# A layer with 32 experts on one core: an expert's further block moves behind its first product, the general path's test moves to expert 29, PSUM banks and the seeding are laid anew

## The chip, the cores and the metric

The kernel runs on one core of a Trainium2 chip. The metric is the device time of one execution in microseconds; before the change the median of three runs is 1111.02 us (1110.48 to 1111.2). PE is TensorE, DVE is VectorE, ACT is ScalarE, POOL is GpSimd, and SP is the engine that here only issues DMAs.

## What is computed

One layer over 256 tokens of width 1024, in float32, with a context prefix of 256 tokens: a modulated norm, one input projection, four mixers side by side, an output projection with a residual (about the first 170 us), and then a mixture of experts. Cut to that second half:

```python
def moe(h, w_router, b_router, w_gu, b_gu, w_down, b_down):
    logits = h @ w_router + b_router
    top_vals, top_idx = lax.top_k(logits, 4)
    gates = jax.nn.softmax(top_vals, axis=-1)
    # for each of 32 experts e, over the tokens that chose it:
    gu = xb @ w_gu[e] + b_gu[e]                     # 1024 -> 2048
    gt = jnp.minimum(gu[:, :1024], 7.0)
    up = jnp.clip(gu[:, 1024:], -7.0, 7.0)
    y = ((up + 1) * gt * jax.nn.sigmoid(1.702 * gt)) @ w_down[e] + b_down[e]   # 1024 -> 1024
    # the sum over a token's four experts, weighted by its gates
x = x + g2 * moe(rmsnorm(x) * (1 + sc2) + sh2)
return rmsnorm(x, final_norm_g)
```

Each expert has 8 MB of `w_gu` and 4 MB of `w_down`, so 402 MB of weights pass through the core once.

## The kernel before

**The stream of weights.** An expert's weights are six units of 2 MB: u0 to u3 are `w_gu`, u4 and u5 are `w_down`. I number units through: unit 6e + u, up to expert 30, whose last unit is sent behind expert 31's first four. A ring of nine places in SBUF holds them. `load_unit` issues a unit's DMA from SP (L571 for `w_gu`, L581 for `w_down`), and `load_to(n)` issues all up to unit n. A unit may be issued when the one nine before it in the same place has been read for the last time; SP waits for that on PE's semaphore, and everything behind it in SP's order waits too. Units 0 to 8 first need what lies in their places from the first half of the kernel: unit 8 takes the place of `XT` and `YT`.

**One expert.** Every expert has room for 64 tokens (CAP). `gate_up(e)` (L961, L972) multiplies the picked tokens by units u0 to u3, two of its eight steps to a unit. `pick` (L930) gathers the next expert's tokens, `swiglu` works on DVE and ACT, `turn_rows` and `turn_act` (L939, L989) transpose, `s_pair` (L923) turns the gates, `scatter_part` (L1026) adds finished rows into the output banks `Y`, and `down(e)` (L961, L998) multiplies by u4 and u5 at the start of the next turn of the loop, L1109 following.

**More than 64 tokens.** `with tc.If(r > CAP)` (L1114) asks in each of the experts 0 to 29, on PE, DVE and ACT, whether there is a further block of 32 tokens; `block` computes it, and reads u0 to u3 (L1057) and u4, u5 (L1075) once more. It stands between `down(e - 1)` and `gate_up(e)`. Where it is skipped, each engine first lets its own earlier work finish and then adds all the counts of the skipped block to its semaphore in one go (on PE 92 of them), so that waits further on mean the same on both ways. With these inputs one expert takes it, expert 8.

**More than 96.** The general path (L1144 to L1169) loads an expert's weights again into six places of the ring and computes blocks until no token is left. Its test (L1149) stands at the end, behind `swiglu()` of expert 31, and it asks SP too. It is not taken here. Where it is skipped, SP waits for the landing of the DMAs whose semaphores it uses, and then adds its counts to them.

**Order and banks.** The order on each engine is that of the code. Before the first expert PE turns `XT` round twice: into banks that ACT scales to `H` (`natural`), and into the output banks `Y` (`seed`), in which the experts' results are then summed. `seed(1)` stands behind `turn_rows` of the first expert and is the last reader of `XT`, so unit 8 waits for it.

Of the kernel before, what the change touches and what calls it, by code (L numbers as in the profile page):

```python
# [9 lines left out]
AF = mybir.ActivationFunctionType  # L10
# [4 lines left out]
P = 128  # L15
D = 1024
# [6 lines left out]
MORE = 32  # L23
SLOT = 2048
# [45 lines left out]
def tile_hybrid_moe(tc, x, ctx, vec, mats, const, pos_col, pos_row, rows, bias, w_mod, w_in, w_out,  # L70
# [4 lines left out]
    with tc.tile_pool(name="big", bufs=1) as big, tc.tile_pool(name="acc", bufs=1, space=PSUM) as acc_pool, \  # L75
# [10 lines left out]
        def R(off, n):  # L86
            return B[:, off:off + n]
# [691 lines left out]
        N = [[bank[4 + 2 * c + q] for q in range(2)] for c in range(2)]  # L779
        Y = [[bank[2], bank[3]], [bank[6], bank[7]]]  # L780
# [7 lines left out]
        jk = R(O_ACC, 512)  # L788
        GT = R(O_GATE, 64).rearrange("p (c e) -> p c e", c=2)
# [15 lines left out]
        def natural(i):  # L805

            for c in range(2):
                pe.transpose(N[c][i // 4][:, (i % 4) * P:(i % 4 + 1) * P], XT[:, i, c * P:(c + 1) * P], ident)

        def seed(c):  # L810

            for i in range(KT):
# [7 lines left out]
        def squares(b, q, a, z):  # L820
            for c in range(2):
                act.activation(jk[:, a:z], N[c][q][:, a:z], AF.Square, scale=D ** -0.5, accum_out=ssq[:, b, c:c + 1])
# [8 lines left out]
        squares(0, 0, 0, 512)  # L831
# [5 lines left out]
        squares(1, 1, 0, 256)  # L837
# [10 lines left out]
        w2 = ssq[:, 0, :]  # L848
        dve.tensor_tensor(out=w2, in0=w2, in1=ssq[:, 2, :], op=ALU.add)
        rsqrt_newton(rs2, w2, tn2)  # L850
        act.activation(SM[:, 1:2], epsc, AF.Exp)
        for c in range(2):
            dve.scalar_tensor_tensor(LG[:, c, :], LR[:, c, :], rs2[:, c:c + 1], LB, op0=ALU.mult, op1=ALU.add)
            for q in range(2):
                act.activation(H[:, c, cols2[q]], N[c][q], AF.Copy, scale=rs2[:, c:c + 1])
            dve.max(out=M8[:, c, :], in_=LG[:, c, :])
        dve.tensor_scalar(nm, M8[:, :, 0], -1.0, None, op0=ALU.mult)
        dve.memset(M8[:, :, TOPK:8], 3.0e38)
        for c in range(2):
            dve.match_replace(out=MK[:, c, :], in_to_replace=M8[:, c, :], in_values=LG[:, c, :], imm_value=-3.0e38)  # L860
            act.activation(EX[:, c, :], LG[:, c, :], AF.Exp, bias=nm[:, c:c + 1])
        dve.tensor_tensor(out=MK, in0=MK, in1=LG, op=ALU.not_equal)
        dve.tensor_copy(MB, MK)
# [42 lines left out]
        G0, G1 = bank[4], bank[5]  # L906
        mis = [bank[0], bank[1]]
# [28 lines left out]
        def turn_rows(dst, ps):  # L936
# [4 lines left out]
            d4 = dst.rearrange("p j (g s) -> p j g s", g=2)  # L941
            dve.tensor_tensor(out=d4, in0=ps.rearrange("p (j g s) -> p j g s", j=4, g=2),  # L942
                              in1=jg(A2s).unsqueeze(3).to_broadcast([P, 4, 2, CAP]), op=ALU.mult)
            dve.tensor_tensor(out=d4, in0=d4, in1=jg(SH2s).unsqueeze(3).to_broadcast([P, 4, 2, CAP]), op=ALU.add)
# [139 lines left out]
        one_hot(0)  # L1084
# [18 lines left out]
        load_to(NPAIR)  # L1103

        parts = [(0, 0), (0, 1), (1, 0), (1, 1)]
        for e in range(NE - 1):
            pr, par = divmod(e, 2)
            if e < NE - 2:
                r = nc.values_load(CNT[0:1, e:e + 1], min_val=0, max_val=L, engines=engines)  # L1109
# [3 lines left out]
            if e < NE - 2:  # L1113
                with tc.If(r > CAP):  # L1114
                    block(e, CAP, G0, G1, GH, TH, UP)
# [5 lines left out]
            gate_up(e, XET)  # L1121
            if e == NE - 2:
                load_to(NE * NUN)
# [24 lines left out]

        with tc.If(r > CAP + MORE):  # L1149
            kept = dict(wt), dict(dn)  # L1150
            for e in range(NE):
                base = CAP if e >= NE - 2 else CAP + MORE
                r = nc.values_load(CNT[0:1, e:e + 1], min_val=0, max_val=L, engines=more)
                with tc.If(r > base):
                    for u in range(NUN):
                        load_unit(3 + u, e, u)
                    for b in range(base, L, MORE):
                        args = e, b, mis[0], mis[0], R(O_O, 512), R(O_O + 512, 512), R(O_XET, 512)
                        if b == base:
                            block(*args)  # L1160
                        else:
                            with tc.If(r > b):
                                block(*args)
            for now, old in zip((wt, dn), kept):
                now.update(old)
# [143 lines left out]
```

## Time and profile before

| | |
|---|---|
| median of three runs | 1111.02 us |
| the profiled execution, its own time | 1112.09 us |
| its span, first to last instruction | 1110.3 us |
| PE busy | 1025.7 us (92%) |
| DMA, mean over the span | 401 GB/s |
| read from HBM | 442.41 MB |

The page gives each engine's busy time, the span in 40 slices and the costliest groups of instructions. PE's 92% is a sum over overlapping matmuls and no proof that PE is the bound: a matmul of 512 columns in float32 is booked with about 0.6 us and the next one starts 0.21 us later. For this kernel the DMA line of the slices, the waits of SP and the timeline around single events tell more.

### The profile page before, as it was taken

Reading aid. Unit: us, or ns where it says so; the run is one execution under the profiler, and the core shown is the slowest. Engines: PE = TensorE matmul, PEld = TensorE weight load, DVE = VectorE, ACT = ScalarE, POOL = GpSimd, SP = SyncE. Lnnn points to the kernel's source line nnn. Section 1 sums busy time; section 2 is a strip of 40 time slices with the busy share of each in tenths; the row PEclk is TensorE's granted clock in tenths of the full one; section 3 lists DMA queues with packets and bytes.
Section 4 is the critical chain, followed back from the end, with each engine's and each line's share of the span. In section 5 each row is a group of like instructions: output and inputs, shape, how many; then the busy total and the mean of one; then the engine's idle time right before and its main releaser. Section 6 shows DMA issues by size and latency. Waiting matters only on the chain. (4 is left out here: it accounts for less than half of the span.)

```text
span 1110.3 us, 11952 instructions
## 1 busy us (share of the span) xinstructions
PE 1025.7 (92%) x4932; PEld 435.8 (39%) x4932; DVE 305.6 (28%) x593; ACT 128.5 (12%) x239; POOL 34.6 (3%) x77
## 2 busy tenths in 40 slices
PE   4999988999999989999999999999989898988896
PEld 2665865333333333333333333333333333323333
DVE  5488742121212222121212121212111212111113
ACT  4133430000000000000000000000000000000002
POOL 4102120000000000000000000000000000000000
PEclk8999998999999989999999999999999999999998
DMA  9997888999999998999999999999999999999992
GB/s 298 375 358 314 338 380 333 403 426 426 426 428 424 426 415 357 428 426 427 426 426 426 425 429 425 427 426 426 429 427 424 427 427 428 424 427 427 427 422 119
DMA packets 42098, 445.59 MB, mean 401 GB/s; under 512 B 4676, under 2 KB 6660, under 8 KB 15240
## 3 DMA queue, kind: packets, MB, share of 16 engines
q1 hardware_dynamic: 41352, 443.43, 95.5%
q8 instruction: 80, 1.31, 0.5%
q0 software_dynamic: 640, 0.63, 0.2%
q14 instruction: 26, 0.21, 0.0%
HBM read 442.41 MB, written 1.05 MB: 399 GB/s over the span
## 5 line engine op out<-in xcount | busy, mean ns | idle before, releaser
L972 PE MATMUL bank<-B 128*64 128x512 f32 x2048 | 457.7, 600 | 19.3 <-DMA B<-in_w_gu_dram 18.9
L972 PEld LDWEIGHTS bank<-B 128*64 128x64 f32 x2048 | 167.3, 138 | 290.8 <-issue 242.1
L998 PE MATMUL bank<-B 128*64 128x512 f32 x992 | 222.1, 600 | 2.8 <-PEq L1149 2.8
L976 DVE TENSOR_SCALAR B<-bank 128x512 f32<-128x512 f32 x32 | 22.1, 692 | 455.7 <-issue 403.3
L998 PEld LDWEIGHTS bank<-B 128*64 128x64 f32 x992 | 70.2, 138 | 135.1 <-issue 129.6
L977 ACT ACTIVATE B<-B 128x512 f32<-128x512 f32 x32 | 20.2, 631 | 754.1 <-DVE B L976 754.1
L1022 DVE TENSOR_TENSOR B<-bank,B 64x512 f32<-64x512 f32 x62 | 42.7, 689 | 212.1 <-PE bank L998 211.4
L1026 PE MATMUL bank<-B 128*128 128x512 f32 x136 | 69.1, 616 | 1.2 <-DVE B L1079 1.1
L930 PE MATMUL bank<-B 128*64 128x512 f32 x256 | 61.5, 592 | 0.9 <-DVE B L866 0.9
L961 PE MATMUL bank<-T,E 96*64 96x512 bf16 x190 | 33.4, 394 | 25.4 <-PEq L1114 20.6
L384 PE MATMUL bank<-B 128*128 128x256 f32 x160 | 37.2, 387 | 0.0
L1026 PEld LDWEIGHTS bank<-B 128*128 128x128 f32 x136 | 22.2, 190 | 36.2 <-issue 23.0
L961 PEld LDWEIGHTS <-E 96*64 96x64 bf16 x190 | 10.5, 106 | 65.3 <-issue 64.6
L930 PEld LDWEIGHTS bank<-B 128*64 128x64 f32 x256 | 20.7, 137 | 35.1 <-issue 33.4
L384 PEld LDWEIGHTS bank<-B 128*128 128x128 f32 x160 | 31.1, 195 | 8.3 <-issue 4.3
L942 DVE TENSOR_TENSOR B<-bank,B 128x512 f32<-128x512 f32 x32 | 22.1, 692 | 30.2 <-PE bank L939 30.2
L939 PEld LDWEIGHTS bank<-B 128*128 128x128 f32 x128 | 19.9, 202 | 17.1 <-ACT B L934 16.8
L990 ACT ACTIVATE B<-bank 128x512 f32<-128x512 f32 x32 | 19.1, 597 | 51.6 <-PE bank L989 51.6
L978 DVE TENSOR_SCALAR B<-bank 128x512 f32<-128x512 f32 x32 | 22.1, 691 | 5.3 <-PE bank L972 5.2
L934 ACT ACTIVATE B<-bank 128x512 f32<-128x512 f32 x32 | 19.1, 597 | 38.1 <-PE bank L930 38.1
L539 DVE SCALAR_TENSOR_TENSOR B<-B 128x256 f32<-128x256 f32 x58 | 23.2, 478 | 0.0
L980 DVE SCALAR_TENSOR_TENSOR B<-B 128x512 f32<-128x512 f32 x32 | 22.1, 692 | 3.3
(302 smaller groups left out, 558.9 us busy)
## 6 DMA issues: line engine op xcount, KB each, us to landing
B<-in_w_gu_dram SPq DMA_DIRECT2D x128, 2048.0 KB, 25.9
B<-in_w_down_dram SPq DMA_DIRECT2D x63, 2048.0 KB, 28.8
B<-in_w_mod_dram SPq DMA_DIRECT2D x16, 1024.0 KB, 6.6
B<-in_w_mod_dram SPq DMA_DIRECT2D x16, 512.0 KB, 10.5
B<-in_w_out_dram SPq DMA_DIRECT2D x4, 1024.0 KB
B<-in_w_in_dram SPq DMA_DIRECT2D x8, 384.0 KB, 6.7
B<-in_w_in_dram SPq DMA_DIRECT2D x8, 256.0 KB, 5.1
B<-in_w_down_dram SPq DMA_DIRECT2D x2, 1024.0 KB
```

The costliest lines, as they stand in the source:

```text
L384: pe.matmul(half(b, t), w, UT[:, k, 256:512], start=(k == 0 and t == 0), stop=(k == KT - 1 and t == 1))
L539: dve.scalar_tensor_tensor(dst, src, w, dst, op0=ALU.mult, op1=ALU.add)
L930: pe.matmul(mis[0][64 * g:64 * g + 64, :], p[:, c, :], H[:, c, 512 * g:512 * g + 512], start=(c == 0), stop=(c == 1))
L942: dve.tensor_tensor(out=d4, in0=ps.rearrange("p (j g s) -> p j g s", j=4, g=2), in1=jg(A2s).unsqueeze(3).to_broadcast([P, 4, 2, CAP]), op= ...
L961: pe.matmul(dst[64 * g:64 * g + 64, :], E3[:, e:e + 1].to_broadcast([96, CAP]), T[:, col:col + 512], start=True, stop=False)
L972: pe.matmul(dst[64 * g:64 * g + 64, :], xt[:, k % 4, (k // 4) * 64:(k // 4) * 64 + 64], w[:, b * 1024 + g * 512:b * 1024 + g * 512 + 512], ...
L976: dve.tensor_scalar(GH, G0, 7.0, 0.5, op0=ALU.min, op1=ALU.mult)
L978: dve.tensor_scalar(UP, G1, 7.0, -7.0, op0=ALU.min, op1=ALU.max)
L980: dve.scalar_tensor_tensor(UP, TH, 1.0, UP, op0=ALU.add, op1=ALU.mult)
L998: pe.matmul(dst[64 * g:64 * g + 64, :], AT[:, k % 4, (k // 4) * 64:(k // 4) * 64 + 64], dn[e, k, g], start=False, stop=(k == KT - 1))
L1022: dve.tensor_tensor(out=dst[p0:p0 + 64, 512 * g:512 * g + 512], in0=ps[64 * g:64 * g + 64, :], in1=G2B[64 * g:64 * g + 64, :], op=ALU.mult)
L1026: pe.matmul(Y[c][q][:, a:b], s[:, c * P:(c + 1) * P], o[:, 512 * q + a:512 * q + b], start=False, stop=last)
```

## The change

Four things are changed. The further block is asked for behind the rest of an expert's turn, and so behind `gate_up(e)` and before `down(e)`. The general path becomes a function that is called at expert 29, between `down(28)` and `gate_up(29)`, with ten loads (units 183 and up) still behind it in SP's order. The banks are assigned anew. Ahead of the first expert the seeding and some of the router's steps stand earlier, the eviction of the first tokens is cut into two parts, and `gate_up(0)` takes its steps in the order in which these become ready.

```diff
+GENERAL = NE - 3
-        N = [[bank[4 + 2 * c + q] for q in range(2)] for c in range(2)]
-        Y = [[bank[2], bank[3]], [bank[6], bank[7]]]
+        N = [[bank[4 + 2 * c], half(5, c), half(7, c)] for c in range(2)]
+        Y = [[bank[2], bank[3]], [bank[0], bank[7]]]
...
-        def seed(c):
+        def seed(c, tiles_):
...
+        squares(2)
+        seed(0, range(4))
         act.activation(LT, bank[0][:, 0:256], AF.Copy)
-        dve.scalar_tensor_tensor(ssq[:, 0, :], ssq[:, 0, :], EPS, ssq[:, 1, :], op0=ALU.add, op1=ALU.add)
+        w2 = ssq[:, 0, :]
+        dve.scalar_tensor_tensor(w2, w2, EPS, ssq[:, 1, :], op0=ALU.add, op1=ALU.add)
+        dve.tensor_tensor(out=w2, in0=w2, in1=ssq[:, 2, :], op=ALU.add)
...
-        squares(2, 1, 256, 512)
-        seed(0)
+        seed(0, range(4, KT))
+        seed(1, range(4))
         rsqrt_newton(rs2, w2, tn2)
...
+        dve.tensor_tensor(out=MB, in0=MK, in1=LG, op=ALU.not_equal)
+        dve.tensor_tensor(out=MK, in0=MK, in1=LG, op=ALU.not_equal)
+        dve.tensor_scalar(nm, M8[:, :, 0], -1.0, None, op0=ALU.mult)
         act.activation(SM[:, 1:2], epsc, AF.Exp)
...
-        G0, G1 = bank[4], bank[5]
-        mis = [bank[0], bank[1]]
+        G0, G1 = bank[5], bank[6]
+        mis = [bank[4], bank[1]]
...
-            for k in range(KT):
+            for k in (0, 1, 4, 5, 2, 3, 6, 7) if e == 0 else range(KT):
...
-        one_hot(0)
+        strided()
+        for i in range(2):
+            dve.tensor_tensor(out=PP[0][:, :, i, :], in0=iota[:, 0:CAP].unsqueeze(1).to_broadcast([P, 2, CAP]),
+                              in1=PM[:, :, i:i + 1].to_broadcast([P, 2, CAP]), op=ALU.is_equal)
+        pick(PP[0][:, :, 0, :])
+        picked()
+        strided_cols()
         gates(0)
         gates(1)
...
-        pick(PP[0][:, :, 0, :])
-        picked()
-        strided()
-        strided_cols()
-        turn_rows(XET, mis[1])
-        seed(1)
+        seed(1, range(4, KT))
+        turn_rows(XET, mis[1], 2)
...
+        def general(at):
+            first = at * NUN + NPAIR - NUN
+            r = nc.values_load(CNT[0:1, NE:NE + 1], min_val=0, max_val=L + MORE, engines=more)
+            with tc.If(r > CAP + MORE):
...
+                        for u in range(NUN):
+                            load_unit(first + u, e, u)
...
+                for i in range(first, first + NUN):
+                    load_unit(i, *stream[i])
...
             if e > 0:
                 down(e - 1, mis[1])
                 load_to(e * NUN + NPAIR)
-            if e < NE - 2:
-                with tc.If(r > CAP):
-                    block(e, CAP, G0, G1, GH, TH, UP)
+            if e == GENERAL:
+                general(e)
...
             if par == 0 and e + 2 < NE:
                 one_hot(pr + 1)
                 gated(pr + 1)
+            if e < NE - 2:
+                with tc.If(r > CAP):
+                    block(e, CAP, G0, G1, GH, TH, UP)
         e = NE - 1
-        more = engines + [ENG.SP]
-        r = nc.values_load(CNT[0:1, NE:NE + 1], min_val=0, max_val=L + MORE, engines=more)
         down(e - 1, mis[1], range(4))
         gate_up(e, XET)
         swiglu()
-        with tc.If(r > CAP + MORE):
...
```

Three places show how instructions stand in a row.

The first is PE around the skip of expert 1's block. Before: `s_pair` (L923), the count's load (L1109), `down(0)` (L961, L998), the branch (L1114), and then the block (L1042 and on).

```order
L923 MATMUL bank_75<-B 128x128 x2
L1109 TENSOR_LOAD CNT
L1109 ISA x2
L961 LDWEIGHTS E_65
L961 MATMUL bank_71<-T,E_65 64x512
L961 LDWEIGHTS E_65
L961 MATMUL bank_71<-T,E_65 64x512
L998 MATMUL bank_71<-B 64x512 x16
L1114 COMPARE_AND_BRANCH
L1042 MATMUL bank_70<-B 32x256 x8
```

After, for expert 0: the end of `gate_up(0)` (now L983), the count's load (L1149), `pick`, the transposes and `s_pair` (L938, L947, L1000, L931), the branch (L1187), the block (L1053 and on).

```order
L983 MATMUL bank_75<-B 64x512 x2
L983 MATMUL bank_76<-B 64x512 x2
L1149 TENSOR_LOAD CNT
L1149 ISA x2
L938 MATMUL bank_74<-B 64x512 x4
L947 MATMUL bank_71<-B 128x128 x4
L1000 MATMUL bank_74<-B 128x128 x4
L931 MATMUL bank_76<-B 128x128 x2
L1187 COMPARE_AND_BRANCH
L1053 MATMUL bank_74<-B 32x256 x8
```

The block's reads of u0 to u3 stood ahead of `gate_up`'s and now stand behind them, so the last read of these places is the block's.

The second is SP at the general path, with the semaphores that each instruction waits for (DMAHW0 to DMAHW7 are those of landings). Before, the end of the program: the skip (L1149) and the two output DMAs.

```order
L1162 COMPARE_AND_BRANCH
L1162 UNCONDITIONAL_BRANCH x2
L1154 UNCONDITIONAL_BRANCH [waits DMAHW0_49,DMAHW1_49,DMAHW2_49,DMAHW3_49,DMAHW4_49,DMAHW6_49,DMAHW7_49]
L1149 UNCONDITIONAL_BRANCH [waits SP_sequencer_49,DMAHW0_49,DMAHW1_49,DMAHW2_49,DMAHW3_49,DMAHW4_49,DMAHW6_49,DMAHW7_49]
L1215 DMA out_dram<-B 128x1024 [waits DMAHW6_49,DVE_49]
L1220 DMA out_dram<-B 128x1024 [waits DMAHW7_49,DVE_49,Activation_49]
```

After, the skip is L1126:

```order
L1126 UNCONDITIONAL_BRANCH
L1126 UNCONDITIONAL_BRANCH [waits SP_sequencer_49,DMAHW0_49,DMAHW1_49,DMAHW2_49,DMAHW4_49,DMAHW5_49,DMAHW6_49,DMAHW7_49]
L1187 UNCONDITIONAL_BRANCH
L572 DMA B<-in_w_gu_dram 128x4096 [waits DMAHW4_49,PE_49]
L582 DMA B<-in_w_down_dram 128x4096 [waits DMAHW5_49,PE_49]
L572 DMA B<-in_w_gu_dram 128x4096 [waits DMAHW6_49,PE_49]
L572 DMA B<-in_w_gu_dram 128x4096 [waits DMAHW7_49,PE_49]
L572 DMA B<-in_w_gu_dram 128x4096 [waits DMAHW0_49,PE_49]
L572 DMA B<-in_w_gu_dram 128x4096 [waits DMAHW1_49,PE_49]
L582 DMA B<-in_w_down_dram 128x4096 [waits DMAHW2_49,PE_49]
```

The skip's wait for landings had only the output behind it; now weight loads stand behind it. The first of its semaphores in that order, DMAHW0 to DMAHW2, belong to units 179, 180 and 181, and DMAHW4 comes behind these.

The third is PE in `gate_up(29)`, its last two units. Before:

```order
L972 MATMUL bank_74<-B 64x512 [waits DMAHW5_49]
L972 MATMUL bank_74<-B 64x512
L972 MATMUL bank_75<-B 64x512 x2
L972 MATMUL bank_74<-B 64x512 x2
L972 MATMUL bank_75<-B 64x512 x2
L972 MATMUL bank_74<-B 64x512 [waits DMAHW6_49]
L972 MATMUL bank_74<-B 64x512
```

After:

```order
L983 MATMUL bank_75<-B 64x512 [waits DMAHW5_49]
L983 MATMUL bank_75<-B 64x512
L983 MATMUL bank_76<-B 64x512 x2
L983 MATMUL bank_75<-B 64x512 x2
L983 MATMUL bank_76<-B 64x512 x2
L983 MATMUL bank_75<-B 64x512 [waits DMAHW6_49,DMAHW4_49]
L983 MATMUL bank_75<-B 64x512
```

The step that reads unit 177 waited for that unit alone (DMAHW6) and now waits for DMAHW4 too, at the value that the skip on SP adds.

## Rows read from the trace of the kernel before

**Rows 1.** The page: rate of the DMA in the 40 slices of the span.

```profile
GB/s 298 375 358 314 338 380 333 403 426 426 426 428 424 426 415 357 428 426 427 426 426 426 425 429 425 427 426 426 429 427 424 427 427 428 424 427 427 427 422 119
```

**Rows 2.** Stretches: busy time of PE, PEld, DVE, ACT, POOL, PEclk, DMA share, GB/s.

```profile
164.00:169.00 5.00, 4.39 (x33) 3.01 (x29) 2.15 (x9) 0.60 (x1) 0.95 (x1) 1.00 0.04 15
...
416.00:420.00 4.00, 4.00 (x22) 1.36 (x20) 0.00 (x0) 0.00 (x0) 0.00 (x0) 1.00 0.18 78
```

**Rows 3.** Waits of SP's queue: us in total, times, longest.

```profile
SPq L571 <- PE bank L972: 190.5, 47, 29.2
```

**Rows 4.** Timeline ahead of the first expert: start, us, instruction, [idle before <-releaser].

```profile
158.46 1.28 ACT L851 ACT_TABLE_LOAD   x1
...
167.06 0.69 DVE L944 TENSOR_TENSOR B<-B 128x512 f32<-128x512 f32 x1
```

**Rows 5.** Timeline of PE, experts 0 to 2.

```profile
166.13 1.95 PE L813 MATMUL bank<-B 128*128 128x128 f32 x16
...
170.45 15.81 PE L972 MATMUL bank<-B 128*64 128x512 f32 x64
...
191.25 0.44 PE L923 MATMUL bank<-B 128*128 128x128 f32 x2 [1.36 <-DVE B L918]
...
201.32 13.93 PE L972 MATMUL bank<-B 128*64 128x512 f32 x64
...
219.57 7.09 PE L998 MATMUL bank<-B 128*64 128x512 f32 x32
```

**Rows 6.** SP's issues of units 9 and 13, and unit 13 from issue to landing.

```profile
175.99 0.33 SPq L571 DMA_DIRECT2D B<-in_w_gu_dram  x1
...
197.34 0.33 SPq L571 DMA_DIRECT2D B<-in_w_gu_dram  x1
...
DMA to landing us min/median/max: 7.8/7.8/7.8
```

**Rows 7.** Timeline around the block of expert 8: PE, and SP's issue of unit 57.

```profile
382.90 7.09 PE L998 MATMUL bank<-B 128*64 128x512 f32 x32
389.92 1.07 PE L1042 MATMUL bank<-B 128*32 128x256 f32 x16
...
415.57 0.62 PE L961 MATMUL bank<-T,E 96*64 96x512 bf16 x4
...
419.67 0.33 SPq L571 DMA_DIRECT2D B<-in_w_gu_dram  x1
```

**Rows 8.** PE's waits behind the skip of the block: us in total, times, longest.

```profile
PE bank L961 <- PEq L1114: 20.6, 27, 2.2
```

**Rows 9.** Timeline of PE, experts 29 to 31, and the end.

```profile
1024.96 3.65 PE L972 MATMUL bank<-B 128*64 128x512 f32 x16 [1.23 <-DMA B<-in_w_gu_dram]
...
1033.03 7.09 PE L998 MATMUL bank<-B 128*64 128x512 f32 x32
...
1054.32 3.65 PE L972 MATMUL bank<-B 128*64 128x512 f32 x16 [1.24 <-DMA B<-in_w_gu_dram]
...
1064.45 3.60 PE L998 MATMUL bank<-B 128*64 128x512 f32 x16
...
1068.32 14.12 PE L972 MATMUL bank<-B 128*64 128x512 f32 x64
1085.21 5.35 PE L998 MATMUL bank<-B 128*64 128x512 f32 x16 [2.78 <-PEq L1149]
...
1093.87 5.35 PE L1011 MATMUL bank<-B 128*64 128x256 f32 x48
```

**Rows 10.** SP: issue of unit 181, its way to landing, and the general path's test and counts.

```profile
1007.14 0.33 SPq L571 DMA_DIRECT2D B<-in_w_gu_dram  x1
...
DMA to landing us min/median/max: 37.4/37.4/37.4
...
L1149 SPq EVENT_SEMAPHORE  x8: 17/17/17, 1065.6 to 1091.3; - x8
...
L1149 SPq COMPARE_BRANCH  x1: 45/45/45, 1060.5 to 1060.5; - x1
```

More of the change, by code (lines that the diff above doesn't have):

```diff
@@ L788, in tile_hybrid_moe @@
         jk = R(O_ACC, 512)
+        W8 = rt[:, 470:486].rearrange("p (c e) -> p c e", c=2)
+        dve.memset(W8, 3.0e38)
         GT = R(O_GATE, 64).rearrange("p (c e) -> p c e", c=2)
@@ L807, in natural @@
             for c in range(2):
-                pe.transpose(N[c][i // 4][:, (i % 4) * P:(i % 4 + 1) * P], XT[:, i, c * P:(c + 1) * P], ident)
-        def seed(c):
-            for i in range(KT):
+                dst = N[c][0][:, i * P:(i + 1) * P] if i < 4 else N[c][i // 2 - 1][:, (i % 2) * P:(i % 2 + 1) * P]
+                pe.transpose(dst, XT[:, i, c * P:(c + 1) * P], ident)
+        def seed(c, tiles_):
+            for i in tiles_:
                 pe.matmul(Y[c][i // 4][:, (i % 4) * P:(i % 4 + 1) * P], XT[:, i, c * P:(c + 1) * P], ident,
@@ L836, in tile_hybrid_moe @@
         natural(5)
-        squares(1, 1, 0, 256)
+        squares(1)
         for i in (6, 7):
@@ L841, in tile_hybrid_moe @@
             logits(k)
+        squares(2)
+        seed(0, range(4))
         act.activation(LT, bank[0][:, 0:256], AF.Copy)
-        dve.scalar_tensor_tensor(ssq[:, 0, :], ssq[:, 0, :], EPS, ssq[:, 1, :], op0=ALU.add, op1=ALU.add)
+        w2 = ssq[:, 0, :]
+        dve.scalar_tensor_tensor(w2, w2, EPS, ssq[:, 1, :], op0=ALU.add, op1=ALU.add)
+        dve.tensor_tensor(out=w2, in0=w2, in1=ssq[:, 2, :], op=ALU.add)
         for c in range(2):
             pe.matmul(LR[:, c, :], LT[:, c * P:(c + 1) * P], E32, start=True, stop=True)
-        squares(2, 1, 256, 512)
-        seed(0)
-        w2 = ssq[:, 0, :]
-        dve.tensor_tensor(out=w2, in0=w2, in1=ssq[:, 2, :], op=ALU.add)
+        seed(0, range(4, KT))
+        seed(1, range(4))
         rsqrt_newton(rs2, w2, tn2)
+        for c in range(2):
+            dve.scalar_tensor_tensor(LG[:, c, :], LR[:, c, :], rs2[:, c:c + 1], LB, op0=ALU.mult, op1=ALU.add)
+            for (a, z), src in zip(((0, 512), (512, 768), (768, 1024)), N[c]):
+                act.activation(H[:, c, a:z], src, AF.Copy, scale=rs2[:, c:c + 1])
+            dve.max(out=M8[:, c, :], in_=LG[:, c, :])
+        for c in range(2):
+            dve.tensor_copy(W8[:, c, 0:TOPK], M8[:, c, 0:TOPK])
+            dve.match_replace(out=MK[:, c, :], in_to_replace=W8[:, c, :], in_values=LG[:, c, :], imm_value=-3.0e38)
+        dve.tensor_tensor(out=MB, in0=MK, in1=LG, op=ALU.not_equal)
+        dve.tensor_tensor(out=MK, in0=MK, in1=LG, op=ALU.not_equal)
+        dve.tensor_scalar(nm, M8[:, :, 0], -1.0, None, op0=ALU.mult)
         act.activation(SM[:, 1:2], epsc, AF.Exp)
         for c in range(2):
[L853 to L860, printed above, removed]
             act.activation(EX[:, c, :], LG[:, c, :], AF.Exp, bias=nm[:, c:c + 1])
-        dve.tensor_tensor(out=MK, in0=MK, in1=LG, op=ALU.not_equal)
-        dve.tensor_copy(MB, MK)
         def gates(c):
@@ L939, in turn_rows @@
                 pe.transpose(ps[:, j * P:(j + 1) * P], cols, ident)
[L941 to L944, printed above, removed]
+            d4, s4 = dst.rearrange("p j (g s) -> p j g s", g=2), ps.rearrange("p (j g s) -> p j g s", j=4, g=2)
+            n = 4 // parts_
+            for j in range(0, 4, n):
+                col = lambda ap: jg(ap)[:, j:j + n].unsqueeze(3).to_broadcast([P, n, 2, CAP])
+                dve.tensor_tensor(out=d4[:, j:j + n], in0=s4[:, j:j + n], in1=col(A2s), op=ALU.mult)
+                dve.tensor_tensor(out=d4[:, j:j + n], in0=d4[:, j:j + n], in1=col(SH2s), op=ALU.add)
         def strided():
@@ L1103, in tile_hybrid_moe @@
         load_to(NPAIR)
+        more = engines + [ENG.SP]
+        def general(at):
+            first = at * NUN + NPAIR - NUN
+            r = nc.values_load(CNT[0:1, NE:NE + 1], min_val=0, max_val=L + MORE, engines=more)
+            with tc.If(r > CAP + MORE):
+                kept = dict(wt), dict(dn)
+                for e in range(NE):
+                    base = CAP if e >= NE - 2 else CAP + MORE
+                    r = nc.values_load(CNT[0:1, e:e + 1], min_val=0, max_val=L, engines=more)
+                    with tc.If(r > base):
+                        for u in range(NUN):
+                            load_unit(first + u, e, u)
+                        for b in range(base, L, MORE):
+                            if b == base:
+                                block(e, b, G0, G1, GH, TH, UP)
+                            else:
+                                with tc.If(r > b):
+                                    block(e, b, G0, G1, GH, TH, UP)
+                for i in range(first, first + NUN):
+                    load_unit(i, *stream[i])
+                for now, old in zip((wt, dn), kept):
+                    now.update(old)
         parts = [(0, 0), (0, 1), (1, 0), (1, 1)]
@@ L1107, in tile_hybrid_moe @@
             pr, par = divmod(e, 2)
-            if e < NE - 2:
-                r = nc.values_load(CNT[0:1, e:e + 1], min_val=0, max_val=L, engines=engines)
+            count = lambda: nc.values_load(CNT[0:1, e:e + 1], min_val=0, max_val=L, engines=engines)
+            if 0 < e < NE - 2:
+                r = count()
             if e > 0:
@@ L1121, in tile_hybrid_moe @@
             gate_up(e, XET)
+            if e == 0:
+                r = count()
             if e == NE - 2:
@@ L1147, in tile_hybrid_moe @@
         swiglu()
-        with tc.If(r > CAP + MORE):
[L1150 to L1165, printed above, removed]
         e = NE - 1
```

9 lines of the change are left out of this document (4 added, 5 removed).

## The prediction

> **What bounds the kernel now.** I began with the 40 slices. From the ninth slice to the last but one the DMA moves 415 to 429 GB/s, with one dip to 357 [rows 1]. A unit is 2.097 MB, and at 427 GB/s that is 4.91 us, so an expert's six units are 29.5 us. Then I asked what PE needs for an expert when it does not wait: from `down(1)` at 219.57 [rows 5] to `down(7)` at 382.90 [rows 7] lie six experts, 163.33 us, 27.2 us each. PE is thus the faster by some 2 us an expert, and the stream of weights sets the time. SP's waits agree on how: its loads of `w_gu` wait for places, 47 times on `gate_up`'s reads [rows 3], which is a full ring and no loss as long as DMAs stay queued.
>
> A change then counts where it stops the stream. Before, it stops in three places. At the start: from 164 to 169 the DMA's share is 0.04 [rows 2], and unit 9 is issued only at 175.99, when `gate_up(0)`, begun at 170.45, has read the first unit [rows 5, 6]. At expert 8: PE is in the block from 389.92 to 415.57 and reads no further place free, unit 57 is issued at 419.67 [rows 7], and from 416 to 420 the DMA's share is 0.18 [rows 2]. The slices of 415 and 357 GB/s are 27.76 us each and lack (12 + 70)/427 of it: 5.3 us lost [rows 1]. At the end: PE waits 2.78 us for the skip of the general path and then runs 16 matmuls in 5.35 us that take 3.60 us elsewhere [rows 9].
>
> **The change part by part.** All sums stand against the profiled execution, 1112.09 us, span 1110.3; the median of the runs is 1.07 less.
>
> *Which instruction frees a place.* This carries the forecast. Units u0 to u3 of expert e were read last by `gate_up(e)`. Now the block's reads come behind it in the code, and where the block is skipped the counts for these reads are added in the skip, behind `s_pair`. The loads into these four places no longer go out one by one during `gate_up` but together behind the skip. From unit u3's landing to the skip I count 3.65 us to read it [rows 9], 4.4 us from its end at 1028.61 to `down` at 1033.03 [rows 9], and 0.76 us for the skip, the mean of 27 [rows 8]: 8.8 us. An issue into an empty queue lands 7.8 us later, as unit 13's did [rows 6]. The place of u0 receives the next expert's u3, so from u3 to u3 the loop needs at least 16.6 us, against 29.5 of the stream: it keeps streaming, but the lead that PE can build up shrinks to 29.5 - 16.6 = 12.9 us. Places of `w_down` are freed as before.
>
> *Start.* The seeding, 1.95 us, leaves the place ahead of `gate_up(0)`, with it the 2.37 us from its end at 168.08 to 170.45, in which the count and the branch stand [rows 5]. That is 4.3 us, so `gate_up(0)` begins at about 166.1. The tokens' eviction, which ends at 167.75 now, must come earlier for that: the table load of 1.28 us goes behind the scaling of `H`, and the first half of the last 0.69 us suffices to begin [rows 4]. If these bring nothing, it begins at 168. Then follow `gate_up(0)`, 13.93 to 15.81 us [rows 5], say 14.9; 5.4 us to the end of `s_pair`, from 186.26 to 191.69 [rows 5]; and the skip, 0.5 to 0.8. Unit 9 goes out at about 187.0 instead of 175.99, 11 us later, although the first product begins earlier. Of these 11, something is lost already: from unit 9's landing (183.8) to unit 13's (197.34 + 7.8 = 205.1) [rows 6] are 21.3 us for four units, 1.7 above 4 x 4.91. The stream starts 9 us later: **+9** (from +5, with 13.93 us, a landing at 7.8 and an even earlier begin, to +13, with a begin at 168 and 15.81 us). What hid the seeding's and the branch's cost before was nothing; what hides the gain now is the late release.
>
> The Trainium skill, "DMA: Bandwidth & Descriptors", section on the anatomy of one DMA, gives 2.0 us plus the bytes over 436 GB/s, which makes 6.8 us of a unit; it speaks of GpSimd's path, the loads here are SP's, and the row says 7.8. By its figure this term and the next would be about 1 us smaller each, the sum 28 instead of 30.
>
> *The block of expert 8.* With it PE needs 27.2 + 25.6 = 52.8 us [rows 7], 23.3 more than the stream. What covers it is PE's lead, at most 12.9 us, and it starts from nothing at expert 1 and grows by about 1.9 an expert (29.5 - 27.2, less 0.4 for the count's load and the skip now both standing between `s_pair` and `down`), so it is about at its cap by expert 8. Lost are 10.4 us, or 13.5 if the lead has grown by only 1.4 each. I take 12, less the 5.3 of now: **+7** (+4 to +10).
>
> *The general path at expert 29.* SP's skip waits for landings: its eight counts stretch from 1065.6 to 1091.3 behind a test at 1060.5 [rows 10]. Now ten loads stand behind such a skip, and among what it waits for are units 179 to 181. So unit 183 goes out after 181 has landed, and `gate_up(29)`'s last two steps wait for the same. Before, 181 landed at 1007.14 + 37.4 = 1044.54 [rows 10], and the last product ended at 1099.22 [rows 9], 54.7 us later. After, from that landing, PE is the chain: the last unit of `gate_up(29)` 5.35 (as 16 matmuls after an idle time take; 3.65 at best); 4.4 + 0.8 to `down(29)`; 7.1 and 0.4; `gate_up(30)` 13.95; 6.5 from its end to `down(30)`, as from 1057.97 to 1064.45; 3.9 from 1064.45 to 1068.32; `gate_up(31)` 14.1; the second half of `down(30)` 3.6, with no skip in front; and 8.7 from there to the end, as from 1090.56 to 1099.22. Sum 68.8, or **+14** (12 to 16) [rows 9]. It holds the gain at the end, 2.8 + 1.75. The loads do not interfere: from 183's landing at +8 they come each 4.9 us, and the last, 191, at +47.
>
> *Free.* The new banks and the order of steps in `gate_up(0)` move no work onto the path: no wait for a bank shows there. The added instructions of DVE and ACT ahead of the first expert lie within the start's bounds.
>
> Sum: 9 + 7 + 14 = +30: 1142.1 by the profiled execution, **1141** by the median.
>
> **The rivals.** *A, not slower.* If the loads are let go during `gate_up` as now, and the test on SP finds its landings done, the start gains the 5.0 us hole and most of the 1.7 and 1.5 behind it, some 8 us, and the end 2.8 + 1.75: -12.5, about 1098. For it speaks that the written purpose of the counts is bookkeeping; against it that the last reader in PE's order is now in the block, and that a skip adds its counts where it stands. It decides by whether SP's issues follow `gate_up`'s steps. *B, the general test is free*: units 179 to 181 have landed when SP gets there, or nothing behind needs it. Then +9 + 7 - 4.5 = +11.5, 1122.5. Against it: SP stands nine units ahead, so units just issued are still 37.4 us from landing [rows 10]. *C, each skip costs more than 0.76 us.* The skip now lies between two products and in front of the releases; the longest before was 2.2 us [rows 8]. At +1 us an expert the lead grows by 0.9 each, is 6 at expert 8 and is never rebuilt to its cap; the block then loses 17 instead of 12: 1146. From +2 on PE is slower than the stream, and each further us costs 22 behind the block: +2.5 gives up to 1163.
>
> The Trainium skill, "Runtime: NRT & Kernel Launch", section on instruction fetch, says that a taken branch to a target outside the fetched window stalls the engine until that is loaded. The rows of before show such a price only as the mean of 0.76; by the rule it would be the same jump in another place, unless the block's code has another length.
>
> **How the numbers follow.** The forecast has 0.66, C 0.17, B 0.10, A 0.07. The forecast's own bounds are +21 to +39, but its three ends are not met together: 1134 to 1149. The range reaches down to B and up into C, 1122 to 1153; left out are A, a little of B and the far end of C, about 0.15. A measurement of this kernel tells about 0.2% from no change. Only A is faster, 0.07; between A and B almost nothing lies, 0.02 for the same; 0.91 slower.
>
> **What would show it.** In the changed kernel's trace: `gate_up(0)` begins near 166; SP issues units 9 to 12 together near 187, and so for every expert, four in a row behind `s_pair`; behind expert 8 the DMA rests 10 to 14 us; PE waits 15 to 20 us in `gate_up(29)`, and from then on the DMA's rate falls, with the last weights landed 20 us ahead of the end. Issues spread over `gate_up` would make the first term wrong, a `gate_up(29)` without a wait the third; many PE waits behind the skip of over 1.5 us would speak for C.

## The result and the profile after

The changed kernel takes 1150.49 us (1145.24 to 1151.72), the kernel before 1111.02. The ratio of the means, which takes in a further run of 1149.88 us, is 1.0346, with an interval of 1.0307 to 1.0385. The profiled execution is the fastest one, 1145.24 us with a span of 1143.5, 33.2 us over that of before. The other timed runs are 4.6 to 6.5 us above it, and I have no trace of those; what follows explains the 33.2.

The page of the changed kernel, the rate in the 40 slices (28.6 us each) and the three groups of matmuls of an expert (count, then busy time and mean ns of one, then idle time before them with what ended it):

```profile
GB/s 304 383 353 320 336 382 189 424 363 429 426 425 428 425 422 408 249 427 419 421 427 428 427 425 428 427 424 427 422 420 428 426 427 426 426 426 424 267 429 121
...
L983 PE MATMUL bank<-B 128*64 128x512 f32 x2048 | 450.3, 595 | 11.0 <-SPq L1126 10.6
...
L1009 PE MATMUL bank<-B 128*64 128x512 f32 x992 | 242.0, 637 | 6.6 <-issue 6.6
...
L971 PE MATMUL bank<-T,E 96*64 96x512 bf16 x190 | 36.0, 411 | 62.3 <-PEq L1187 43.8
```

Three slices fall most: 189 at the start, 249 at expert 8's block, 267 at the general path, where the kernel before has 333, 357 and no dip [rows 1]. So far this is the forecast. A fourth, 363 where the kernel before has 426, stands at expert 2 and was not in it. And the second and third of the groups hold something that it did not: PE idles 62.3 us ahead of the bias of `down`, nearly all of it behind the skip (L1187), and `down`'s matmuls have become slower, 242.0 us for the 222.1 that the page of before has.

PE's longest waits say how it is distributed (total, times, longest), and the line of the branch itself (its duration, min/median/max in ns):

```profile
PE bank L971 <- PEq L1187: 43.8, 10, 5.8
PE bank L971 <- DVEq L1187: 15.9, 18, 0.9
...
L1187 PEldq COMPARE_BRANCH  x31: 70/337/6405, 184.9 to 1072.9; - x31
```

In most experts the branch takes about 0.34 us and PE loses 0.9 us. In nine it takes 4.7 to 6.4 us, and PE loses 2.6 to 5.9 us each time, 43 us together.

What a long branch waits for stands among the DMA queues, in one whose packets are of the kind "instruction" (packets, MB, share of the DMA engines: first the whole span, then expert 5's branch alone, 330.8 to 336.9 us, then the whole span of x6, an experiment below in which this test stands at expert 8 only):

```profile
q8 instruction: 80, 1.31, 0.5%
...
q8 instruction: 1, 0.02, 1.1%
...
q8 instruction: 41, 0.67, 0.2%
```

In each of the nine long branches one such packet of 16 KB starts, 2.2 to 3.9 us behind the start of the branch, and the branch ends 1.3 to 1.5 us behind the end of the packet; in expert 5 the packet runs from 334.47 to 335.58 and the branch until 336.92. In none of the shorter ones does a packet start. So the long branches are those for which instructions had to be fetched. Three idle times of PE ahead of `down`'s own matmuls, 2.15, 2.22 and 1.59 us, most of the 6.6 above, end 1.4 to 1.7 us behind such a packet too.

The timeline of PE in expert 5, and three stretches (busy times of PE, PEld, DVE, ACT, POOL, then granted clock, DMA share, GB/s):

```profile
331.91 0.38 PE L931 MATMUL bank<-B 128*128 128x128 f32 x2
337.81 0.64 PE L971 MATMUL bank<-T,E 96*64 96x512 bf16 x2 [5.52 <-PEq L1187]
338.23 8.80 PE L1009 MATMUL bank<-B 128*64 128x512 f32 x32
...
332.00:337.00 5.00, 0.29 (x3) 0.05 (x1) 1.00 (x2) 0.87 (x2) 0.00 (x0) 0.80 1.02 429
338.00:346.00 8.00, 8.00 (x30) 2.57 (x30) 0.00 (x0) 0.00 (x0) 0.00 (x0) 0.76 1.00 424
367.00:375.00 8.00, 7.48 (x38) 2.85 (x40) 0.16 (x1) 0.00 (x0) 0.00 (x0) 1.00 1.01 426
```

Behind 5.5 us of idleness `down` runs at a mean granted clock of 0.76, between the levels 1.2 and 2.4 GHz, and takes 8.8 us; in expert 6, behind a short skip, the clock is 1.00 and it takes 7.05.

Now the view that decides: who waited for the weights of `w_gu` from 200 to 1045 us. Before:

```profile
PEld bank L972: 39.6, 26
PE bank L972: 18.9, 19
...
DMA to landing us min/median/max: 9.0/27.1/40.4
```

After, the view has no such row at all. No product of `gate_up` waits for a weight's landing in that time, and none of `down` either; each unit lies in its place when PE comes to it. From `gate_up(10)` at 478.28 to `gate_up(28)` at 1011.96 PE needs 29.65 us an expert, and that is PE's own pace. The stream, where nothing holds it back, needs 29.36 (six landings, 4.893 us apart), so the margin is narrow: the DMA stays nearly full, and what PE lacks is the lead that the forecast gave it. **PE, not the stream, is the bound of the changed kernel.**

SP's issue of unit 9 and its waits for places, and the general path's counts on SP with `gate_up(29)` around them:

```profile
185.76 0.33 SPq L572 DMA_DIRECT2D B<-in_w_gu_dram  x1
...
SPq L572 <- PEq L1187: 565.1, 29, 22.8
...
L1126 SPq EVENT_SEMAPHORE  x8: 17/17/17, 1045.9 to 1065.1; - x8
...
1042.64 11.62 PE L983 MATMUL bank<-B 128*64 128x512 f32 x48
1064.86 5.60 PE L983 MATMUL bank<-B 128*64 128x512 f32 x16 [10.60 <-SPq L1126]
...
1120.20 3.60 PE L1009 MATMUL bank<-B 128*64 128x512 f32 x16
...
1127.11 5.35 PE L1022 MATMUL bank<-B 128*64 128x256 f32 x48
```

SP's loads wait 29 times for PE's skip, as the forecast said, and unit 9 goes out at 185.76. In `gate_up(29)` PE waits 10.6 us for SP's counts, less than the 15 to 20 of the forecast, since PE itself came later. The last product ends at 1132.46.

### The profile page after: what moved, and what is told of

It reads as the page before. It is cut to its first block, busy times and chain, and to the rows that moved or that the text cites. A ratio compares the mean times of both kernels' runs of the same rounds, so it can differ in the third digit from the quotient of the medians.

```text
span 1143.5 us, 11960 instructions
## 1 busy us (share of the span) xinstructions
PE 1030.5 (90%) x4932; PEld 424.7 (37%) x4932; DVE 305.7 (27%) x598; ACT 128.7 (11%) x241; POOL 34.7 (3%) x77
## 5 line engine op out<-in xcount | busy, mean ns | idle before, releaser
L983 PE MATMUL bank<-B 128*64 128x512 f32 x2048 | 450.3, 595 | 11.0 <-SPq L1126 10.6
L983 PEld LDWEIGHTS bank<-B 128*64 128x64 f32 x2048 | 150.4, 138 | 292.7 <-issue 274.8
L1009 PE MATMUL bank<-B 128*64 128x512 f32 x992 | 242.0, 637 | 6.6 <-issue 6.6
L1009 PEld LDWEIGHTS bank<-B 128*64 128x64 f32 x992 | 77.3, 147 | 149.9 <-issue 148.6
L971 PE MATMUL bank<-T,E 96*64 96x512 bf16 x190 | 36.0, 411 | 62.3 <-PEq L1187 43.8
L938 PE MATMUL bank<-B 128*64 128x512 f32 x256 | 62.5, 592 | 0.0
L385 PEld LDWEIGHTS bank<-B 128*128 128x128 f32 x160 | 31.1, 195 | 8.4 <-issue 4.3
L938 PEld LDWEIGHTS bank<-B 128*64 128x64 f32 x256 | 19.1, 137 | 35.9 <-issue 35.8
L953 DVE TENSOR_TENSOR B<-bank,B 128x512 f32<-128x512 f32 (+1 forms) x33 | 22.3, 675 | 30.0 <-PE bank L947 30.0
L947 PEld LDWEIGHTS bank<-B 128*128 128x128 f32 x128 | 20.0, 202 | 17.2 <-ACT B L942 16.8
```

Source lines behind the costliest of these rows:

```text
L385: pe.matmul(half(b, t), w, UT[:, k, 256:512], start=(k == 0 and t == 0), stop=(k == KT - 1 and t == 1))
L938: pe.matmul(mis[0][64 * g:64 * g + 64, :], p[:, c, :], H[:, c, 512 * g:512 * g + 512], start=(c == 0), stop=(c == 1))
L953: dve.tensor_tensor(out=d4[:, j:j + n], in0=s4[:, j:j + n], in1=col(A2s), op=ALU.mult)
L971: pe.matmul(dst[64 * g:64 * g + 64, :], E3[:, e:e + 1].to_broadcast([96, CAP]), T[:, col:col + 512], start=True, stop=False)
L1009: pe.matmul(dst[64 * g:64 * g + 64, :], AT[:, k % 4, (k // 4) * 64:(k // 4) * 64 + 64], dn[e, k, g], start=False, stop=(k == KT - 1))
```

## The experiments

To compare runs whose first weights land up to 2.5 us apart I take four numbers from each trace: the landing of unit 18 after that of unit 2; the stream's loss around expert 8's block (units 53 to 67, less 14 x 4.893 us); PE's time an expert from `gate_up(2)` to `gate_up(7)`; and the time from unit 181's landing to the end of the span. Each comes from one trace. The ratios of the experiments stand against the kernel before as timed beside them (medians of 1109.15 to 1111.88 us).

| kernel | ratio, interval | unit 18 | block | PE an expert | 181 to end |
|---|---|---|---|---|---|
| before | 1 | 89.6 | 5.2 | 27.5 | 65.8 |
| changed | 1.0346 (1.0307 to 1.0385) | 98.5 | 13.3 | 29.5 | 78.8 |
| x1 block back | 1.0175 (1.0147 to 1.0204) | 92.1 | 5.2 | 27.4 | 79.2 |
| x2 general at the end | 1.0247 (1.0218 to 1.0275) | 98.6 | 14.7 | 29.1 | 67.4 |
| x3 both back | 1.0037 (1.0016 to 1.0058) | 92.5 | 4.1 | 27.4 | 66.3 |
| x4 general without SP | 1.0237 (1.0187 to 1.0287) | 97.2 | 13.5 | 29.0 | 67.6 |
| x5 branch, early release | 1.0262 (1.0234 to 1.0289) | 84.9 | 18.4 | 30.1 | 81.9 |
| x6 neither | 0.9951 (0.9926 to 0.9975) | 83.5 | 1.5 | 26.4 | 78.7 |
| x12 late release, no branch | 1.0188 (1.0161 to 1.0216) | 97.9 | 9.3 | 27.2 | 79.8 |
| x10 test inside `down` | 1.0342 (1.0313 to 1.0370) | 102.8 | 13.1 | 28.2 | 79.3 |
| x7 block back, general on POOL | 1.0021 (0.9996 to 1.0046) | 90.5 | 4.7 | 27.7 | 65.5 |
| x8 x3 without expert 0's test | 0.9949 (0.9929 to 0.9969) | 83.3 | 2.8 | 27.1 | 66.6 |
| x9 x7 without expert 0's test | 0.9959 (0.9940 to 0.9978) | 85.5 | 2.4 | 27.0 | 66.1 |
| x13 before without it | 0.9990 (0.9976 to 1.0005) | 86.1 | 4.9 | 27.4 | 66.1 |

**Undoing one part at a time (x1 to x4).** x1 moves the block's test back:

```diff
             if e == GENERAL:
                 general(e)
+            if e < NE - 2:
+                with tc.If(r > CAP):
+                    block(e, CAP, G0, G1, GH, TH, UP)
...
-            if e < NE - 2:
-                with tc.If(r > CAP):
-                    block(e, CAP, G0, G1, GH, TH, UP)
```

> The changed kernel with the further block's test back between down(e - 1) and gate_up(e), for all experts 0 to 29; start, banks and general path as changed. Theory (the late release of u0 to u3 costs the start and the block's term, the general path's wait on SP the rest, and the terms add): unit 9 goes out near 170 instead of 187, the stream starts some 8 us earlier than in the kernel before, the block of expert 8 loses about 5 us as it did there, the general path costs +13: about 1111 - 8 + 13 = 1116 us. Rival (the general path and the start's own changes carry most of the loss, the block's place little): about 1140.

x2 puts the general path's test at the end, in the words of the kernel before.

> The changed kernel with the general path's test back at the end, behind swiglu() of expert 31; the block's test stays late. Theory: the late release keeps its cost (start +9, block +8, some more from PE's longer skips), the 13 us from unit 181's landing on go away: about 1150 - 13 = 1137 us. Rival (the loss is one of PE's longer turn, and with the stream running on to the end PE is no better): 1145 to 1150.

x3 does both.

> The changed kernel with both back: the block's test between down(e - 1) and gate_up(e) and the general path's test at the end; what is left of the change is the start and the banks. Theory: the stream starts some 8 us earlier than in the kernel before and the rest is as there: about 1103 us. Rival (the start's loss of 9 us was the seeding and the order of steps, not the late release): 1111 to 1120.

x4 leaves the general path at expert 29, but asks PE, DVE and ACT alone (`engines=engines`) and has no `load_unit` in it.

> The changed kernel in which the general path at expert 29 asks PE, DVE and ACT alone; its loads on SP are left out, and its blocks would use expert 29's weights. Theory (SP's wait for landings is the term): no wait of PE in gate_up(29), the DMA streams on to the end, and the end has no skip: about 1150 - 13 - 4.5 = 1133 us. Rival (PE's own test and its branch at that place are the term): 1145 to 1150.

Measured, by the medians on their chip: x1 1128, x2 1136, x3 1113, x4 1134, the kernel before 1109. x2 and x4 came out as expected, and they agree: it is SP's wait and not PE's test that costs at expert 29, some 1.0 to 1.1% or 11 to 12 us, and the end is 67.4 and 67.6 us behind unit 181 instead of 78.8. The block's place is worth 1.7%, 19 us. But x1 missed its expectation by 12 us and x3 by 10: with the block's test back the start does not gain. The timeline of PE in x3 ahead of `gate_up(0)` shows why:

```profile
162.62 0.71 PE L947 MATMUL bank<-B 128*128 128x128 f32 x4
165.89 0.41 PE L971 MATMUL bank<-T,E 96*64 96x512 bf16 x2 [2.56 <-DVEq L1129]
169.98 0.64 PE L971 MATMUL bank<-T,E 96*64 96x512 bf16 x2 [3.68 <-issue]
170.41 1.07 PE L983 MATMUL bank<-B 128*64 128x512 f32 x2
```

PE is done with the transposes at 163.33 and stands idle for 2.56 us at the skip of expert 0's block and for 3.68 us with nothing to wait for but its own next instructions. Inside the second of these an instruction packet runs from 167.69 to 168.63, and PE goes on 1.35 us behind its end: a fetch, as in the long branches. In the kernel before the packet runs from 167.91 to 168.92; PE had work until 168.76, most of it `seed(1)` [rows 5], and less of the fetch showed:

```profile
170.21 0.62 PE L961 MATMUL bank<-T,E 96*64 96x512 bf16 x3 [1.45 <-issue]
```

**Release and branch apart (x5, x6, x12).** In x5 the block's first product reads `w_down`'s tiles, so the branch stays where it is and `gate_up` is the last reader of u0 to u3 again.

```diff
-                              wt[e, k][:, 512 * g:512 * g + 512], start=False, stop=(k == KT - 1))
+                              dn[e, k, g % 2], start=False, stop=(k == KT - 1))
```

> The changed kernel in which the further block reads w_down's tiles (units u4, u5) in place of w_gu's in its first product, so that gate_up(e) is again the last reader of u0 to u3; the branch stands where the change put it, and expert 8's block computes with the wrong weights. Theory (the release is the cause, the skip's own length on PE is not): unit 9 goes out near 170, the start gains 8 us against the kernel before, the block loses 5 to 10, the general path 13: 1116 to 1123 us. Rival (PE's branch, which in every third expert takes about 6 us and shows 4 to 6 us of them as idle time of PE in the changed kernel, is the cause, whatever frees the places): 1140 to 1150.

x6 has the test for expert 8 alone (`if e == 8:`).

> The changed kernel with the further block's test left in for expert 8 alone, at its new place; the other experts have neither test nor branch nor a block. Theory: places are freed inside gate_up in 31 experts, only expert 8's are freed late; the start gains 8 us against the kernel before, the block loses 5 to 10, the general path 13: 1116 to 1123 us, within 3 us of the kernel whose block reads w_down's tiles. Rival (the branch on PE costs time by itself): 10 us or more faster than that kernel.

x12 adds to x6 a late reader without a branch:

```diff
+            if e < NE - 2 and e != 8:
+                for u in range(4):
+                    pe.matmul(mis[0][0:32, 0:32], ident[:, 0:32], wt[e, 2 * u][:, 0:32], start=True, stop=True)
             if e == 8:
```

> The kernel with the block's test at expert 8 alone, and in the other experts, where the branch stood, four matmuls of 32 columns on PE that read a corner of u0 to u3 into a bank that nobody reads: the late release alone, without a branch. Theory (the release price of the prediction is right): against the kernel with the test at 8 alone the stream starts 13 us later, and expert 8's block loses about 10 us instead of 1.3: +5 percent of neither branch nor fetch, 1106 + 22 = 1128 us. Rival (with PE's turn at 27 us and no fetch the late release costs the start alone): 1106 + 13 = 1119 us.

My theory fell with x5: 1140.6 us, on the rival's figure, though unit 18 lands 13.6 us earlier than in the changed kernel. And x6, 1106.1, is 3.1% faster than x5, which is the second rival: it lacks 29 of the 30 tests, and only expert 8's places come free later in it than in x5. PE's waits in x5, then in x6 and x12:

```profile
L971 PE MATMUL bank<-T,E 96*64 96x512 bf16 x190 | 36.5, 415 | 62.6 <-PEq L1187 44.3 <-DVEq L1187 15.9 <-PEq L1126 2.3
```

```profile
L983 PE MATMUL bank<-B 128*64 128x512 f32 x2048 | 456.4, 599 | 49.2 <-DMA B<-in_w_gu_dram 31.1 <-SPq L1126 17.6 <-DVE B L954 0.4
```

```profile
L983 PE MATMUL bank<-B 128*64 128x512 f32 x2048 | 458.5, 600 | 52.3 <-DMA B<-in_w_gu_dram 34.9 <-SPq L1126 17.0 <-DVE B L954 0.4
```

Without the branches PE waits for weights (31.1 and 34.9 us): the stream is the bound, as I had assumed it for the changed kernel. In x5, as in the changed kernel, it never does for `gate_up`'s. The four kernels, all with the general path's cost in them, are -0.5% (neither), +1.9% (late release alone), +2.6% (branch alone) and +3.5% (both). Single prices of 2.4 and 3.1% would add up to 5.5%; both together cost 4.0%, more than the larger and clearly less than the sum. The two overlap: with the branch there, the late release adds 0.8% instead of 2.4. x12 alone came out as expected, 1130 for 1128: start 8.3 us later than before and a loss of 9.3 at the block, where the forecast's sum has 9 and 12, or 10.4 with the lead at its cap. So the release price of the forecast was sized about right, in a kernel that has this branch at expert 8 only.

**Covering the branch (x10).** The test moves behind the first half of `down`:

```diff
-                down(e - 1, mis[1])
+                down(e - 1, mis[1], range(4))
+                if e < NE - 1:
+                    with tc.If(r > CAP):
+                        block(e - 1, CAP, G0, G1, GH, TH, UP)
+                down(e - 1, mis[1], range(4, KT))
```

> The changed kernel with the further block's test behind the first half of down(e) instead of ahead of it, so that 3.6 us of matmuls stand in PE's queue when the branch is issued, while the places come free 3.6 us later still. Theory (the part of the branch that PE's queue does not cover makes PE's turn as long as the stream's, so that no lead is left for expert 8's block): PE's waits behind the skip fall from some 60 us to 25, the block loses 8 us or so less, in all about 10 us less than the changed kernel's 39 over the kernel before: 1141. Rival (the release decides, and it is later): 1153 or more.

Half of it happened. PE's time an expert falls to 28.2, PE waits for weights again, and the waits behind the skip fall, though not to 25:

```profile
PE bank L1009 <- PEq L1154: 37.6, 29, 3.2
PE bank L983 <- DMA B<-in_w_gu_dram: 17.2, 17, 1.6
```

But the places come free later (unit 18 at 102.8 for 98.5), the block loses as much as in the changed kernel (13.1 for 13.3), and the time is the same, 1.0342: 1147 us, between the theory's 1141 and the rival's 1153. Inconclusive as a verdict between theory and rival; what it suggests is that one price is bought with the other as long as the test stands behind `gate_up`.

**Towards a faster kernel (x7, x8, x9, x13).** x7 has the block's test back, and the general path at expert 29 issues its loads from POOL (`load_unit(..., pool)`, and POOL in place of SP among the engines that it asks).

> The changed kernel with the block's test back between down(e - 1) and gate_up(e), and the general path at expert 29 with its loads issued by POOL instead of SP, so that SP has no skip there and gate_up(29) waits for no landing beside its own. Theory: the start's gain of 8 us and the end's gain of 4.5 us (no skip of 2.8, no 1.75 of slower matmuls behind it) add up: about 1111 - 12.5 = 1098 us, faster than both kernels. Rival (the end is bound by the last landings anyway): 1103, as with both parts back.

x8 is x3 with expert 0's further tokens left to the general path, which already does that for experts 30 and 31, so that no branch stands ahead of `gate_up(0)`; x9 is the same on x7, and x13 the same on the kernel before:

```diff
+        dve.tensor_tensor(out=cl, in0=cl, in1=CN[0:1, 0:1], op=ALU.max)
...
-            if e < NE - 2:
+            if 0 < e < NE - 2:
                 with tc.If(r > CAP):
...
-                base = CAP if e >= NE - 2 else CAP + MORE
+                base = CAP if e == 0 or e >= NE - 2 else CAP + MORE
```

> The kernel with both parts back (block's test between the products of neighbouring experts, general path at the end), and expert 0's further tokens left to the general path, as experts 30 and 31 have it, so that no branch stands ahead of gate_up(0). Theory (that branch, with 2.6 + 3.7 us of idle PE ahead of gate_up(0), ate the start's gain): gate_up(0) begins near 164, unit 9 goes out near 168 instead of 175.5, the stream is 7 us earlier: 1113 - 7 = 1106 us. Rival (unit 8's landing or the stream's end sets the time anyway): 1111 to 1113.

> The same with the general path at expert 29 and its loads on POOL. Theory: 1114 - 7 = 1107 us; if the end's skip had its price there, 2 to 4 us faster than the kernel with the general path at the end: 1103 us.

> The kernel before with one edit: expert 0's further tokens are left to the general path, as experts 30 and 31 have it, so that no branch stands ahead of gate_up(0); seeding, banks and order of steps as before. Theory (the branch was the larger price at the start, the early seeding the smaller): gate_up(0) begins some 2 us earlier, behind seed(1), unit 9 goes out 4 us earlier, ratio to the kernel before about 0.9965, a little more than the 0.9949 of the same edit on top of the change's start. Rival (the early seeding is worth nothing): 0.995. Rival (the branch was hidden by seed(1)): 1.000.

x7 costs 1.5% less than x1 and no more than x3: the whole price of the general path at expert 29 sat on SP's queue. But it missed its expectation: 1114 us for 1098, or the rival's 1103. The start's gain of 8 us is not there, as in x3, and no gain shows at the end: x7 is not below x3, nor x9 below x8, by more than the intervals, though only x3 and x8 have the skip of some 3 us at the end. That doesn't show that this skip is free. In x9 PE stands 10.63 us at expert 29, where the skips of the general path and of the block now follow each other, and waits for no landing from there on, so what the end may gain is lost there, and the last product starts at the same time (first x8, then x9):

```profile
1077.28 5.30 PE L1009 MATMUL bank<-B 128*64 128x512 f32 x16 [3.07 <-PEq L1164]
...
1085.89 5.35 PE L1022 MATMUL bank<-B 128*64 128x256 f32 x48
```

```profile
1012.62 1.06 PE L972 MATMUL bank<-T,E 96*64 96x512 bf16 x4 [10.63 <-PEq L1160]
...
1079.15 3.60 PE L1010 MATMUL bank<-B 128*64 128x512 f32 x16
...
1086.05 5.35 PE L1023 MATMUL bank<-B 128*64 128x256 f32 x48
```

x8 is faster than both kernels of the case, by 0.5% than the kernel before: 1103.99 us against 1109.39 on the same chip, where 1106 was expected. Its first product starts 24.8 us behind unit 2, as in the changed kernel, instead of 30.6 as in x3:

```profile
163.86 0.62 PE L971 MATMUL bank<-T,E 96*64 96x512 bf16 x4
164.91 13.95 PE L983 MATMUL bank<-B 128*64 128x512 f32 x64 [0.42 <-DVE B L954]
```

x13, the same edit without the early seeding, is within the noise of the kernel before; its theory, 0.9965, lies outside the interval, the second rival's 1.000 inside. Together with x3 and x8 it says that the early seeding pays only where no branch follows it, and the branch's removal pays in full only with the seeding gone from its old place. Its trace has unit 18 3.5 us earlier, the timing shows between 2.7 us less and 0.6 us more than before.

## Why the prediction was right in its number, and where not in its reason

**The start, right.** `gate_up(0)` was to begin near 166.1, and began at 165.93; unit 9 was to go out at 187.0, and went out at 185.76. The stream was to start 9 us later: unit 18 is 8.9 us later. x5 and x6, where `gate_up` frees the places, have 84.9 and 83.5 instead of 98.5, and x12, with a late reader and no branch, 97.9, so the late release is shown to be the cause.

**The general path, right.** From unit 181's landing to the end of the last product I had 68.8 us, an added 14; measured are 1132.46 - 1064.70 = 67.8, an added 13. x2, x4 and x7 show that SP's wait is the cause. Two steps inside were off. Unit 183 did not wait for 181's landing but for expert 29's own skip, and went out at 1074.5; it did no harm, since PE was later still. And the wait of PE in `gate_up(29)` is 10.6 us and not 15 to 20. The 4.5 us that I booked as a gain at the end are in the measured chain: the second half of `down(30)` begins at 1120.20 without a wait and takes 3.60 us. Whether the end's skip can be saved in a faster kernel stays open; x7 and x9 lose more at expert 29 than that.

**The block, right in size and wrong in reason.** I took 12 us for the loss there, from a lead that is capped at 12.9 us; the trace has 13.3. But PE had less than half of that lead. It can be read from the load of u3 of expert 8, the first that the last skip ahead of the block lets go: what its way from issue to landing has above the 7.8 us of an empty queue [rows 6]. In the changed kernel, then in x12, it takes

```profile
DMA to landing us min/median/max: 13.6/13.6/13.6
...
DMA to landing us min/median/max: 20.9/20.9/20.9
```

So the lead was 5.8 us, and in x12, where this branch is gone, 13.1, the forecast's cap. By the forecast's own sum 5.8 would have lost 17.5. That it was 13.3 is in part luck: the turn with the block took 50.5 us instead of the 52.8 that I had, and the next one, behind a short branch, 26.3.

The step that failed is "grows by about 1.9 an expert (29.5 - 27.2, less 0.4 for the count's load and the skip". The skip cost not 0.76 us but (43.8 + 15.9)/28 = 2.1 on average, 1.4 more, and the slower matmuls behind the long ones another (242.0 - 222.1)/31 = 0.6; PE's expert grew by 2 us, from 27.5 to 29.5, and with that PE was on average no faster than the stream. x6, without tests, needs 26.4 us and loses 1.5 at the block, x12 with the lead but late release 9.3, x5 with early release and a lead of 6.2 (14.0 from issue to landing) 18.4.

The mean of 0.76 [rows 8] was a price under cover: before, the branch is issued while `down`'s matmuls still stand in PE's queue. Its own duration in the trace of before is as long at the most, and by the median longer; the fifteen of over 3 us hold an instruction packet each:

```profile
L1114 PEldq COMPARE_BRANCH  x31: 82/2394/6435, 166.8 to 1006.1; - x31
```

With up to 4.4 us of `down` to run beside it, at most 2.2 of these 6.4 us showed. I moved the branch behind `s_pair`, where 1.5 to 3 us are queued, and kept the price from the old place. The Trainium skill, "Runtime: NRT & Kernel Launch", section on instruction fetch, says that a taken branch to a target outside the fetched window forces a fetch before the engine goes on. The trace agrees: the nine long branches of the changed kernel hold the start of an instruction packet each, the shorter ones none. DVE's and ACT's branches at the same tests took 0.05 us. Why PE's target is missing at some experts and not at others, no run here shows.

**The rivals.** C was the one that describes the bound: "From +2 on PE is slower than the stream". It had 0.17, and its condition, many PE waits behind the skip of over 1.5 us, was met. The median of 1150.5 lies above the forecast's own bounds, 1134 to 1149, and among C's values, 1146 to 1163; it is the range, drawn up into C, that holds it. The forecast's late release is real but hidden by the branch for the most part. That the sum of 30 us came close to the traced 33.2 is thus partly luck: the start (8.9), the block (8.1) and the general path (13.0) appear in the stream's own landings whichever engine holds it back. 3.2 remain, 2.5 of them at unit 21, which waited for the long skip of expert 2. What the timed runs have above the profiled one, 4.6 to 6.5 us, stays open. A and B fell: no issue follows `gate_up`'s steps, and the general path has its price.

## What to carry to other kernels

A price read off a wait is a price under the cover of what was queued on that engine; when an instruction is moved, read its own duration and ask what will stand in the queue at its new place. The DMA packets of the kind "instruction" tell whether it waits for a fetch. A test behind the last reader of a buffer is itself a last reader on the way that skips it, and a skip that waits for landings holds whatever stands behind it on the queue. Two causes that hold back the same stream need not add: leave each out by itself before a loss is put down to one.

## What the runs showed of the hardware

A branch on PE that skips a block took mostly 0.34 us and nine times 4.7 to 6.4 us in one run, while DVE's and ACT's took 0.05; in the kernel before most of that lay beside queued matmuls. Each long one ended 1.3 to 1.5 us behind a 16 KB packet of the instruction queue. Behind 5.5 us of PE's idleness the granted clock was 0.76 over the next 8 us and 32 matmuls took 8.8 us instead of 7.05. Such a packet also lies in a stall for which the profile names no wait: ahead of the first expert x3's PE stood 3.68 us, until 1.35 us behind the packet's end.
